# Early bf16 copies of half of w_up, a norm moved to VectorE, FFN state terms moved under mixer tile 2, and a table rule for ScalarE, in a fused decoder layer on 8 cores

## The chip, the cores and the metric

One Trainium2 chip, all 8 cores; each core does one prompt sequence and 16 sample tokens of the batch. The metric is the device time of the slowest core in microseconds. Some executions fall into a slower state in which the cores of a die get a lower clock (972 us here, for a kernel that otherwise takes 830).

## The reference

One layer of a decoder on 2080 tokens per core, width 1024:

```python
h = rmsnorm(x, g_pre_mix);  z = h @ w_in                  # 1024 -> 4096: u, v, B, C, two gates
a = multiscale_pool(u) @ w_pool * scale;  b = (B * causal_dwconv(C * v)) @ w_conv_out
x = x + rmsnorm((sigmoid(ga) * a + sigmoid(gb) * b) @ w_o, g_post_mix)
h = rmsnorm(x, g_pre_ffn)
gate, val = split(causal_dwconv(h @ w_up))                # 1024 -> 5632, state of 2 rows
x = x + rmsnorm((silu(gate) * val) @ w_down, g_post_ffn)
```

Outputs are the tokens and the new states. Weights come in float32 and are used as bf16.

## The kernel before

The kernel runs the mixer over 5 tiles of tokens (0: 512, 1 to 4: 392 columns), then the FFN over 6 tiles of 344 columns. Between them the normalized activations go through DRAM (`h2T`). A Python scheduler lists all operations, orders them for each engine with a model of their durations, and emits fixed instruction streams with semaphores. So a wait on the chip arises where an operation is later than its place in its engine's stream assumes. The norm's sums of squares are small matmuls that the scheduler puts among the others at the time at which it expects their input.

```python
def epi_r(t, q):                       # residual: scale R, add x, square, store y
    ...                                # tiles 0-3: multiply on VectorE, then pool_dma(r, xT.., acc=True)
    act(... Square: XSQ2 <- R)         # tile 4: multiply and add on GpSimd (pool_tt)
    sp_dma(yT[...], R[t]...)           # after every second q
def epi_x(t, k):                       # second norm: h2 = R * g3 * rstd
    if last:                           # tile 4
        act(... r = r * g3, waits for the y store)
        pool_tt(... h = r * rstd)
    else:
        dve(... h = r * g3 * rstd in one scalar_tensor_tensor)
    if k % 4 == 3: sp_dma(h2T[...], H2S[t]...)
def pre_ffn():                         # sample tokens' FFN state terms, at FFN tile 1
    sp_dma(ST_FFN, st_ffn)             # ST_FFN lies over Y
    3 x pool tensor_tensor of 704 columns
def wup(n): ...                        # pool_dma: next n w_up blocks, float32 DRAM -> bf16 SBUF
```

Buffers are laid over each other. What matters below: the residual buffer `R` of tile 1 overlaps that of tile 0, and so does `XSQ2` of tile 1 (its squares), so the output projection of tile 1 (`WO`, evacuated by ScalarE) may not write there before tile 0's `y` store has landed; the FFN's `Y` and `YSQ` lie over tile 4's `R` and `H2S`.

## Time and profile before

| | before |
|---|---|
| fast runs | 829.4 to 831.3 us |
| TensorE busy | 96% of 832.4 us |
| lost by TensorE between 336 and 445 us, mean of 8 cores (largest) | 10.9 us (14.0) |
| the same from 30 to 336 us (mixer) | 0.0 us (0.6) |

"Lost" is used for this sum: for each matmul, the distance from its start to the next one's start, less the usual distance for its width (147 ns at 346 columns, 166 at 392, 210 at 498). It counts waits and half-clock stretches together, in one profiled execution. The page, the stretches, the waits and the chain of the kernel before are shown and read in the prediction.

### The profile page before, as it was taken

The page shows a single profiled execution, that of the slowest core. Times are in us where ns is not written, and L with a number is a line of the kernel's source. Part 1 is how long each engine was busy: PE and PEld are TensorE (multiplying, and loading weights), DVE is VectorE, ACT ScalarE, POOL GpSimd, SP SyncE. Part 2 cuts the span into 40 slices and gives each one's busy share as a digit, 9 for nine tenths or more (in the row PEclk, how much of TensorE's full clock was granted, in tenths as well). Part 3 has the DMA queues.
Part 4 walks back from the last instruction along what each step waited for, and adds up shares of the span by engine and source line. Part 5 has one row for each costly group of instructions (what it writes and reads, how often), then busy time and mean ns, then how long its engine had stood idle before and what let it go on. Part 6 is the DMA issues. An engine that isn't in the chain of part 4 may idle for free.

```text
span 832.4 us, 16714 instructions; the slowest of 8 cores (825.7 to 832.4 us)
## 1 busy us (share of the span) xinstructions
PE 801.2 (96%) x5108; PEld 499.1 (60%) x5108; DVE 556.6 (67%) x1046; ACT 471.8 (57%) x923; POOL 269.0 (32%) x305
## 2 busy tenths in 40 slices
PE   6999999999999999989969999999999999999994
PEld 4455455555555555556646666666666666666662
DVE  2987438876957686578756586658656766685723
ACT  3433386676575646687834475557555654775531
POOL 6432002001002262589662243225212522152231
PEclk9999999999999999999989999999999999999998
DMA  9999706556116999999990033004201500050073
GB/s 171 199 152 157 158 1 154 144 128 140 55 36 155 128 152 196 176 153 168 174 152 1 2 67 37 26 24 62 55 1 35 70 1 1 2 69 2 2 124 82
DMA packets 62838, 75.16 MB, mean 90 GB/s; under 512 B 3072, under 2 KB 59264, under 8 KB 62736
## 3 DMA queue, kind: packets, MB, share of 16 engines
q0 software_dynamic: 41440, 44.97, 39.4%
q1 hardware_dynamic: 21312, 29.14, 13.1%
q8 instruction: 43, 0.70, 0.3%
q14 instruction: 43, 0.35, 0.2%
HBM read 81.53 MB, written 22.90 MB: 125 GB/s over the span
## 4 chain that ended last, share of the span: by engine, by line
PE 88%; DMA 5%; ACT 2%; issue 2%; POOL 2%; DVE 1%; DVEq 0%; ACTq 0%; POOLq 0%; SPq 0%
PE ps L464 88%; DMA big<-xT 2%; DMA h2T<-big 1%; DMA big<-w_up 1%; DVE big L821 1%; POOL big L835 1%; POOL big L477 0%; POOL big L757 0%; ACT big L817 0%; DVEq L1047 0%; DVE big L865 0%; ACT big L941 0%; ACT big L834 0%; ACT big L724 0%; ACT big L848 0%
## 5 line engine op out<-in xcount | busy, mean ns | idle before, releaser
L464 PE MATMUL ps<-big 128*128 128x346 bf16 (+4 forms) x5108 | 801.2, 320 | 19.7 <-ACT big L845 6.5
L464 PEld LDWEIGHTS ps<-big 128*128 128x128 bf16 x5108 | 499.1, 99 | 321.5 <-issue 26.4
L821 DVE SCALAR_TENSOR_TENSOR big<-ps,big 128x344 f32<-128x344 f32 (+1 forms) x528 | 280.4, 569 | 108.5 <-ACT big L817 90.0
L835 POOL TENSOR_TENSOR big<-big 128x344 bf16<-128x344 f32 x132 | 124.9, 949 | 256.5 <-DVE big L821 176.1
L817 ACT ACTIVATE big<-ps,big 128x344 f32<-128x344 f32 (+1 forms) x264 | 138.6, 542 | 65.7 <-PE ps L464 61.2
L834 ACT ACTIVATE big<-big 128x344 f32<-128x344 f32 x132 | 64.3, 489 | 38.5 <-DVE big L821 36.8
L475 POOL DMA_DIRECT2D big<-xT x16 | 15.6, 1011 | 174.7 <-DVE big L707 107.8
L694 ACT ACTIVATE big<-ps 128x392 f32<-128x392 f32 (+1 forms) x80 | 39.0, 514 | 53.4 <-PE ps L464 32.2
L845 ACT ACTIVATE big<-ps,big 128x344 f32<-128x344 f32 x48 | 26.0, 547 | 57.9 <-PE ps L464 55.7
L707 DVE SCALAR_TENSOR_TENSOR big<-ps,big 128x392 f32<-128x392 f32 (+1 forms) x40 | 25.8, 646 | 41.8 <-PE ps L464 41.0
L477 POOL DMA_DIRECT2D big<-w_up x44 | 33.4, 764 | 53.2 <-PE ps L464 47.6
L508 DVE TENSOR_TENSOR big<-big 128x1568 bf16<-128x1568 bf16 (+3 forms) x28 | 22.2, 795 | 31.1 <-ACT big L726 30.1
L475 POOL DMA_DIRECT2D yT<-big x21 | 27.3, 1488 | 32.0 <-DVE big L865 17.2
L851 DVE TENSOR_TENSOR big<-big 128x688 bf16<-128x688 bf16 x17 | 8.8, 517 | 41.9 <-ACT big L848 41.9
L724 ACT ACTIVATE big<-ps,big 128x392 f32<-128x392 f32 (+1 forms) x40 | 24.5, 612 | 17.7 <-PE ps L464 11.1
L848 ACT ACTIVATE big<-ps 128x344 bf16<-128x344 f32 x48 | 21.6, 450 | 18.8 <-PE ps L464 11.1
L603 DVE TENSOR_TENSOR big<-big 128x406 f32<-128x406 f32 (+7 forms) x50 | 30.0, 600 | 3.1 <-ACT big L666 1.1
L477 POOL DMA_DIRECT2D big<-w_in x32 | 23.0, 735 | 21.0 <-DMA big<-w_in 13.5
L575 DVE SCALAR_TENSOR_TENSOR big<-big 128x392 f32<-128x392 f32 (+1 forms) x40 | 25.4, 646 | 2.2 <-ACT big L572 1.6
L713 DVE TENSOR_TENSOR big<-big 128x392 bf16<-128x392 f32 (+1 forms) x40 | 23.1, 587 | 2.4
L711 DVE TENSOR_TENSOR big<-ps,big 128x392 f32<-128x392 f32 (+1 forms) x40 | 23.4, 586 | 1.9 <-ACT big L694 0.4
L572 ACT ACTIVATE big<-big 128x392 f32<-128x392 f32 (+1 forms) x20 | 12.6, 636 | 20.7 <-DVE big L658 20.7
(62 smaller groups left out, 375.6 us busy)
## 6 DMA issues: line engine op xcount, KB each, us to landing
big<-w_up POOLq DMA_DIRECT2D x44, 256.0 KB, 13.1
big<-w_in POOLq DMA_DIRECT2D x32, 256.0 KB, 24.2
yT<-big POOLq DMA_DIRECT2D x21, 344.0 KB, 6.5
big<-xT POOLq DMA_DIRECT2D x16, 392.0 KB, 8.5
yT<-big SPq DMA_DIRECT2D x8, 784.0 KB, 8.7
big<-w_dn POOLq DMA_DIRECT2D x8, 704.0 KB, 20.1
big<-xT SPq DMA_DIRECT2D x6, 784.0 KB, 6.0
big<-h2T SPq DMA_DIRECT2D x6, 692.0 KB, 6.3
```

Source lines behind the costliest of these rows:

```text
L464: ins = e.matmul(o, lhsT=l, rhs=x, start=(start and i == 0), stop=(stop and i == last))
L475: return S.add("pool", lambda e: e.dma_start(out=out, in_=in_, accum_op=ALU.add, max_dma_last_dim=mx), r, w, dma=True, byts=byts, pri=pri, ...
L477: return S.add("pool", lambda e: e.dma_start(out=out, in_=in_, max_dma_last_dim=mx), r, w, dma=True, byts=byts, pri=pri, after=after)
L575: dve(lambda e, k=k: e.scalar_tensor_tensor(out=cv, in0=p[:, 2 + k + lo:2 + k + N], scalar=cc(C_WC + 4 * k + c), in1=cv, op0=ALU.mult, op1 ...
L603: dve(lambda e, nx=nx, cur=cur, s=s, a2=a2: e.tensor_tensor(out=nx[:, a2:W], in0=cur[:, a2:W], in1=cur[:, a2 - s:W - s], op=ALU.add), [ct] ...
L694: act(lambda e, b=b, g=g: e.activation(out=GT[t].ap[:, g, lo:N], in_=bank(b, N, lo), func=AF.Sigmoid), [("ps", b)], [GT[t].t(g, 1)], N, ps ...
L707: dve(lambda e: e.scalar_tensor_tensor(out=A_, in0=bank(bp, N, lo), scalar=cc(C_PS + m), in1=A_, op0=ALU.mult, op1=ALU.mult), [("ps", bp), ...
L817: act(lambda e, b=b, fj=fj, tt=tt: e.activation(out=tt[:, 0:n], in_=bank(b, n), func=AF.Copy, scale=cc(C_WF + fj)), [("ps", b), KCST], [to ...
L821: dve(lambda e, b=b, fj=fj, tt=tt, k=k: e.scalar_tensor_tensor(out=tt[:, 0:n], in0=ps[:, b * 512 + k:b * 512 + k + n], scalar=cc(C_WF + 44 ...
L834: act(lambda e: e.activation(out=g, in_=g, func=AF.Silu), [T.t(0, 1)], [T.t(0, 1)], NB, tab="silu")
L835: S.add("pool", lambda e: e.tensor_tensor(out=gb.ap[:, j, :], in0=g, in1=v, op=ALU.mult), [T.t()], [gb.t(j, 1)], dur=NB * 2.17 + 100)
L845: act(lambda e: e.activation(out=Y.ap[:, m, :], in_=bank(b, NB), func=AF.Copy, scale=cc(C_G4 + m)), [("ps", b), KCST], [Y.t(m, 1)], NB, ps ...
```

## The change

Its intent is to empty the handover from mixer to FFN, where DMA and GpSimd are full, by doing work earlier, where they are idle:

1. 22 of the 44 w_up blocks are cast under tiles 1 to 3 from DRAM to a bf16 scratch in DRAM, and fetched later by SyncE without a cast.
2. Tile 4's second norm goes from ScalarE and GpSimd to VectorE.
3. The FFN state terms are computed under tile 2 instead of FFN tile 1, in another buffer.
4. The scheduler may hold ScalarE up to 0.4 us for an operation of the function table that is loaded (the table rule).

```diff
+NDIR = 22
+                    if c.tab not in (None, tab):
+                        near = [x for x in a if x.tab == tab and ready[x.idx] <= s + 400.0]
+                        if near:
+                            c = min(near, key=lambda x: x.pri + x.off)
+                            s = max(s, ready[c.idx])
...
-    ST_FFN = Buf(Y.off, 44, 2 * NS)
+    ST_FFN = Buf(h2b.off, 44, 2 * NS)
... (in wup: blocks from NDIR on come by sp_dma from wu16)
+    def wcast(n):
+        for _ in range(n):
+            i = cast_next[0]
+            cast_next[0] += 1
+            pool_dma(wu16[:, (i - NDIR) * BL:(i - NDIR + 1) * BL], w_up[:, i * BL:(i + 1) * BL], ...
... (epi_x: the branch for tile 4 is gone; pri=-30000 + 1500 * k if last; epi_n2: flt 6000 -> 2500)
-            if t == NTA - 1:
-                wup(1)
+            if t == L:
+                wup(2)
+            elif t > 0 and m > t and cast_next[0] < 44:      # gates of tiles 1 to 3
+                wcast(1)
...
+    pre_ffn_load()                                           # after the gates of tile 1
     for t in range(2, L):
         for i in range(16):
             F_block(t, i)
+            if i % 2 == 0 and i < 10:                        # projection of tiles 2 and 3
+                wcast(1)
... 
         B(t)
+        if t == 2:
+            pre_ffn()
```

More of the change, by code (lines that the diff above doesn't have):

```diff
@@ L303, in build_nc @@
     h2T = nc.dram_tensor("h2T", [128, KC, NTOK], BF16).ap()
+    wu16 = nc.dram_tensor("wu16", [128, (44 - NDIR) * KC * 128], BF16).ap()
     stack = ExitStack()
@@ L425, in build_nc @@
     H2, G = [h2a, h2b], [g0, g1]
-    ST_FFN = Buf(Y.off, 44, 2 * NS)
-    assert ST_FFN.end <= Y.end
+    ST_FFN = Buf(h2b.off, 44, 2 * NS)
+    assert ST_FFN.end <= PRE.off and R[1].end <= ST_FFN.off + 1600
     TAIL = Buf(h2a.off, 1, 44 * 18)
@@ L492, in wup @@
             k = i + 1
-            while k < hi and W_UP.b[k].off == W_UP.b[k - 1].off + BW:
+            while k < hi and k != NDIR and W_UP.b[k].off == W_UP.b[k - 1].off + BW:
                 k += 1
             dst = Buf(W_UP.b[i].off, 1, (k - i) * BL, True)
-            pool_dma(dst.flat, w_up[:, i * BL:k * BL], [], [dst.t()], 128 * (k - i) * BL * 4, mx=2048,
+            if i < NDIR:
+                pool_dma(dst.flat, w_up[:, i * BL:k * BL], [], [dst.t()], 128 * (k - i) * BL * 4, mx=2048,
+                         after=[last_pe[0]])
+            else:
+                j = i - NDIR
+                sp_dma(dst.flat, wu16[:, j * BL:(j + k - i) * BL], [("wu", b) for b in range(i, k)], [dst.t()],
+                       128 * (k - i) * BL * 2, after=[last_pe[0]])
+            i = k
+    cast_next = [NDIR]
+    def wcast(n):
+        for _ in range(n):
+            i = cast_next[0]
+            cast_next[0] += 1
+            pool_dma(wu16[:, (i - NDIR) * BL:(i - NDIR + 1) * BL], w_up[:, i * BL:(i + 1) * BL], [], [("wu", i)], 128 * BL * 4, mx=2048,
                      after=[last_pe[0]])
-            i = k
     def load_x(t, parts, after=()):
@@ L769, in epi_n2 @@
     def epi_n2(t):
-        rstd(XSQ2[t], 0 if t == NTA - 1 else 2, TA[t], lo_of(t, LO), flt=6000.0 if t == NTA - 1 else 4000.0)
+        rstd(XSQ2[t], 0 if t == NTA - 1 else 2, TA[t], lo_of(t, LO), flt=2500.0 if t == NTA - 1 else 4000.0)
     def epi_x(t, k):
@@ L776, in epi_x @@
         r, h = R[t].ap[:, k, lo:N], H2S[t].ap[:, k, lo:N]
-        if last:
-            act(lambda e: e.activation(out=r, in_=r, func=AF.Copy, scale=cc(C_G3 + k)),
-                [R[t].t(k, 1), KCST, ("y", t, k // 4)], [R[t].t(k, 1)], N, ap=1)
-            pool_tt(lambda e: e.tensor_tensor(out=h, in0=r, in1=SD.ap[:, rs, lo:N], op=ALU.mult),
-                    [R[t].t(k, 1), SD.t(rs, 1)], [H2S[t].t(k, 1)], N)
-        else:
-            dve(lambda e: e.scalar_tensor_tensor(out=h, in0=r, scalar=cc(C_G3 + k), in1=SD.ap[:, rs, lo:N],
-                                                 op0=ALU.mult, op1=ALU.mult),
-                [R[t].t(k, 1), SD.t(rs, 1), KCST], [H2S[t].t(k, 1)], N, stt=True)
+        dve(lambda e: e.scalar_tensor_tensor(out=h, in0=r, scalar=cc(C_G3 + k), in1=SD.ap[:, rs, lo:N],
+                                             op0=ALU.mult, op1=ALU.mult),
+            [R[t].t(k, 1), SD.t(rs, 1), KCST], [H2S[t].t(k, 1)], N, stt=True, pri=-30000 + 1500 * k if last else 0)
         if k % 4 == 3:
@@ L882, in epi_y, with pre_ffn_load @@
                      2 * 128 * 2 * NB * 4, acc=True, mx=4096)
+    def pre_ffn_load():
+        sp_dma(ST_FFN.flat, st_ffn_d, [], [ST_FFN.t()], 128 * 1408 * 4, after=[last_pe[0]])
     def pre_ffn():
-        sp_dma(ST_FFN.flat, st_ffn_d, [], [ST_FFN.t()], 128 * 1408 * 4)
         st = ST_FFN.flat.rearrange("p (c r s) -> p c r s", c=44, r=2)
@@ L890, in pre_ffn @@
         S.add("pool", lambda e: e.tensor_tensor(out=st[:, :, 0, :], in0=st[:, :, 0, :], in1=w0b, op=ALU.mult),
-              [ST_FFN.t(), KCST], [ST_FFN.t()], dur=du)
+              [ST_FFN.t(), KCST], [ST_FFN.t()], dur=du, after=[last_pe[0]])
         S.add("pool", lambda e: e.tensor_tensor(out=st[:, :, 1, :], in0=st[:, :, 1, :], in1=w1b, op=ALU.mult),
-              [ST_FFN.t(), KCST], [ST_FFN.t()], dur=du)
+              [ST_FFN.t(), KCST], [ST_FFN.t()], dur=du, after=[last_pe[0]])
         S.add("pool", lambda e: e.tensor_tensor(out=PRE.ap, in0=st[:, :, 0, :], in1=st[:, :, 1, :], op=ALU.add),
@@ L953, in build_nc @@
         F_block(t, i)
+    L = NTA - 1
     def B(t):
@@ L970, in epi @@
             epi_x(t, k)
-    L = NTA - 1
     B(0)
@@ L987, in build_nc @@
         B(t)
+        if t == 2:
+            pre_ffn()
+    assert cast_next[0] == 44
     for i in range(16):
@@ L1012, in build_nc @@
         if t == 1:
-            pre_ffn()
             assert up_next[0] == 44
```

## The prediction

> **What bounds the kernel now.** I read the page first, then busy time by stretches of 20 us, then TensorE's own waits, then the chain of waits around the worst one. The page says that TensorE is busy 96% of the span, with one dent in the clock it was granted:
>
> ```profile
> span 832.4 us, 16714 instructions; the slowest of 8 cores (825.7 to 832.4 us)
> PE 801.2 (96%) x5108; PEld 499.1 (60%) x5108; DVE 556.6 (67%) x1046; ACT 471.8 (57%) x923; POOL 269.0 (32%) x305
> PEclk9999999999999999999989999999999999999998
> ```
>
> So TensorE is the bound, and only its holes can be won. The stretches show where they are (columns: TensorE, weight loads, VectorE, ScalarE, GpSimd busy us, granted clock, DMA share, GB/s):
>
> ```profile
> 320.00:340.00 20.00, 20.00 (x123) 11.90 (x122) 12.42 (x22) 11.36 (x19) 8.29 (x12) 1.00 1.08 192
> 340.00:360.00 20.00, 19.26 (x130) 12.28 (x128) 13.13 (x26) 16.24 (x30) 8.85 (x12) 1.00 1.09 150
> 360.00:380.00 20.00, 17.84 (x122) 11.52 (x121) 15.13 (x32) 14.29 (x29) 19.68 (x20) 1.00 1.13 154
> 380.00:400.00 20.00, 19.37 (x133) 12.74 (x131) 18.49 (x37) 13.69 (x28) 19.13 (x18) 1.00 1.15 172
> 400.00:420.00 20.00, 19.46 (x131) 12.64 (x132) 15.13 (x31) 17.25 (x35) 13.90 (x16) 1.00 1.07 192
> 420.00:440.00 20.00, 13.48 (x79) 8.17 (x78) 8.36 (x16) 6.81 (x15) 10.73 (x10) 0.83 0.86 111
> ```
>
> From 30 to 340 us (mixer tiles) and from 440 to 780 us (FFN) every stretch is full. Holes are in the start, the last 12 us, and in 340 to 440 us, where the mixer hands over to the FFN: idle there is 0.74 + 2.16 + 0.63 + 0.54 + 6.52 = 10.6 us. After the 6.5 us hole the clock records give half speed for 6.8 us, of which TensorE worked 6.2, so some 3.1 us more are lost: 13.7 us. Summing the matmuls' start distances in the trace over the median distance of their own width gives 14.0 us for this core, and 13.1, 8.9, 9.5, 7.7, 11.7, 8.4, 14.0 for cores 0 to 6. The waits in this stretch:
>
> ```profile
> PE ps L464 <- ACT big L845: 6.5, 1, 6.5
> PE ps L464 <- DMA big<-w_up: 1.6, 1, 1.6
> PE ps L464 <- DVE big L821: 1.3, 4, 0.5
> PE ps L464 <- DVE big L508: 0.6, 1, 0.6
> ```
>
> The longest one, followed back in the chain (start us, us, what) and on ScalarE:
>
> ```profile
> 416.27 0.99 POOL big L780
> ...
> 417.38 12.47 DMA h2T<-big
> ```
>
> ```profile
> 429.93 0.46 ACT L848 ACTIVATE big<-ps 128x344 bf16<-128x344 f32 x1 [7.69 <-DMA h2T<-big]
> ```
>
> L848 is the square that evacuates the first down-projection. It writes a buffer that lies over tile 4's second normalized tile, so it must wait until that tile is stored to DRAM. The store waits for L780, the eight GpSimd multiplies of about 1.0 us that run between 409.7 and 425.0, interleaved with the FFN's own GpSimd products; the second half's store goes out at 425.1 and lands at 429.9. ScalarE stands behind it, PSUM fills, TensorE stops. GpSimd is busy 38.8 of the 40 us before (360 to 400): it is the slow link of the whole tile-4 epilogue.
>
> **What the Trainium skill says.** "TensorE: Matmul & The Clock Gate", section "Part 1: The HAM clock gate", says that the clock falls to half after an idle window of about 3.4 us and returns after a busy one. The trace agrees: hole of 6.52 us, half clock for 6.8 us. Thus removing this hole is worth more than its length. "DMA: Bandwidth & Descriptors", section "SWDGE vs HWDGE vs iDMA", says that a cast during DMA must be issued by GpSimd and that plain copies can go from SyncE; here all casting weight loads are indeed GpSimd issues of about 0.74 us each. "ScalarE: Activation LUTs", section "What ACT_TABLE_LOAD costs", gives 1283 ns for a load; the trace shows 1.28 us.
>
> **The change, part by part.**
>
> *Weights.* 22 of the 44 w_up blocks are cast early into DRAM and fetched by SyncE as bf16. Removed from the GpSimd queue around 300 to 380 us: 22 x 0.74 = 16 us of issue, of which about 7 x 0.74 = 5 us lie in the crowded 360 to 380 us. For DMA: the GpSimd queue moved 44.97 MB in 39.4% of 832 us, 7.3 us of all 16 engines per MB; the SyncE queue 29.14 MB in 13.1%, 3.7 us per MB. 22 blocks of 0.262 MB are 5.8 MB, so 42 us leave the saturated stretch (share 1.07 to 1.15) and 22 come back. Also the loads are issued two at a time in tile 4, so the last ones no longer race the pairs that use them. The 1.6 us wait for w_up (with its neighbours 2.5 us in 360 to 372) goes. Added: 22 casts under tiles 1 to 3. Between 110 and 275 us the DMA share is 0.45, 74 us of 165; plus 42 it is about 0.7. TensorE is full there and has no load to wait for; nothing lies on the path unless the accumulating loads of the residual come late.
>
> *Second norm of tile 4 on VectorE.* Removed: 8 x 1.0 us GpSimd and 8 x 0.62 us ScalarE (L778, which also wait for the y store). Added: the same operation as in the other tiles, 0.622 us each on VectorE by line L783, 8 x 0.622 = 5.0 us, with priority, beside an FFN in which VectorE is busy 18.5 of 20 us (380 to 400).
>
> *State terms.* Three GpSimd products (1.4 + 1.4 + 1.7 = 4.4 us, at 422.7 to 433.5) and a 704 KB load leave the FFN for tile 2, where GpSimd is busy about a tenth of the time. They also leave the region of Y, so Y no longer waits on them.
>
> *Table rule.* After a Ln, the scheduler now waits up to 0.4 us for an Exp of the same table instead of switching. In the first tile-4 norm this saves two loads:
>
> ```profile
> 353.42 1.28 ACT L519 ACT_TABLE_LOAD   x1
> ...
> 356.20 1.28 ACT L834 ACT_TABLE_LOAD   x1
> ...
> 359.25 1.28 ACT L524 ACT_TABLE_LOAD   x1
> ```
>
> With the Exp right after the Ln (which ends at 355.3) the scale is ready at about 355.9 instead of 361.1, 5 us sooner.
>
> *Sum on the path of the hole.* The store that ended at 429.9 comes earlier by 5 us (table rule) + about 5 (weight issues gone from GpSimd) + the L780 stretch, 15.3 us, shrinking to some 6 on VectorE = some 19 us: it lands near 411. The first square was ready to run at 422.2 (429.9 less its wait of 7.69), and by the other holes' 4 us sooner, 418. The margin is 7 us, so I take it that this hole and its half-clock tail go entirely: 6.7 + 2.1 on the slowest core. Of the 14.0 us lost I expect to stay: 1.2 at the entry to the FFN (PSUM waits behind ScalarE's evacuation at 342 to 352, untouched), 0.5 elsewhere, and about 1.5 new, from the VectorE burst: 3.2. Cores' spans less their own loss give a floor of 818.1 to 820.0 (the highest is core 4: 831.7 - 11.7). The slowest core then ends at about 819.7 + 3.2 = 822.9 in the profile; the timed median is 1.1 below the profiled span (831.3 against 832.4), so about 822.
>
> **Rivals.** (1) *VectorE takes over as the bound of the hand-over.* In FFN tile 0 a pair of blocks takes TensorE 16 x 147 ns = 2.35 us and VectorE four times about 0.53 = 2.1 us; 5 us of extra work with priority meets a slack of a tenth, and the PSUM buffers hold some three pairs, 7 us. For: 18.5 of 20 us busy. Against: the items are spread by their priorities, and by 400 to 420 us VectorE is at 15.1. It would leave 4 to 6 us of holes: 825 to 827. (2) *The casts disturb the mixer.* Each sum of squares of a norm stands at a fixed place in TensorE's order, set for expected latencies; a cast of 1.9 us ahead of the accumulating residual load (8.5 us from issue to landing) could hold TensorE a few us per tile: 826 to 832. For: same queue, in order. Against: the casts sit in the first part of each tile and the DMA share stays under 1. (3) *The store's wait is replaced by another*, such as w_dn, which lands 20.1 us after issue, or SyncE loads held in its in-order queue ahead of y and h2 stores. W_dn gains from the emptier queue, so I give it little: 824 to 828. (4) *Everything is hidden*: 818 to 819.
>
> **Range and chances.** All of the gain lies inside 14 us, 1.7% of 831; over 2% would need under 814.7 and some 4 us from the start or the end, which the change doesn't touch. Slower by 2% would need 848, that is holes in the mixer larger than all those of today. I put 822, with 818 to 828 as the range.
>
> **What would show it right or wrong.** Right: in 340 to 440 us TensorE idles under 4 us, the clock stays 1.00 past 30 us, no ScalarE wait for the h2 store near 420 remains, table loads fall below 45, and the GpSimd share in 360 to 400 drops well below 19 of 20. Rival 1: TensorE waits for L821 summing to over 3 us, with the new norm before them on VectorE. Rival 2: stretches between 110 and 340 us with TensorE under 20.00, waiting for a norm's tree sum. Wrong altogether if the span stays above 829, or if TensorE's hole near 427 is still there with another releaser.

## The result

832.41 us median (830.4 to 832.6, 4 runs, all fast) against 830.75 us (four runs, one of them slow; the three fast ones have a median of 830.2): a ratio of 1.002, 95% interval 0.9996 to 1.0044. Ratios here are the mean time of one kernel's fast runs over that of the other's fast runs of the same rounds, so not quite the ratio of the quoted medians. The kernel is no faster; I had predicted 822, with 828 as the upper end. The page after:

```profile
span 831.1 us, 16766 instructions; the slowest of 8 cores (823.0 to 831.1 us)
PE 799.8 (96%) x5108; PEld 498.3 (60%) x5108; DVE 568.1 (68%) x1054; ACT 451.5 (54%) x902; POOL 259.7 (31%) x294
PEclk9999999999999999999999999999999999999998
```

The dent in the granted clock is gone from the page, and yet TensorE's share is the same. The stretches of the slowest core, 4 (same columns as in the prediction):

```profile
160.00:180.00 20.00, 18.30 (x109) 10.38 (x107) 18.90 (x34) 7.33 (x14) 0.04 (x1) 1.00 1.29 159
180.00:200.00 20.00, 16.14 (x80) 8.75 (x81) 7.75 (x14) 13.91 (x28) 0.00 (x0) 0.83 0.71 161
...
220.00:240.00 20.00, 17.55 (x107) 10.18 (x106) 19.31 (x30) 7.20 (x16) 5.67 (x6) 1.00 0.99 158
...
360.00:380.00 20.00, 20.00 (x138) 13.31 (x136) 16.66 (x34) 15.96 (x30) 14.34 (x13) 1.00 0.25 85
380.00:400.00 20.00, 20.00 (x139) 13.35 (x137) 18.38 (x35) 14.52 (x29) 19.57 (x18) 1.00 1.03 155
400.00:420.00 20.00, 18.98 (x130) 12.46 (x129) 19.14 (x38) 14.06 (x27) 10.42 (x12) 1.00 1.14 191
420.00:440.00 20.00, 20.00 (x138) 13.36 (x137) 16.67 (x32) 10.84 (x23) 6.32 (x8) 1.00 0.55 101
```

The handover is nearly full: one hole of 1.0 us is left, and 420 to 440 us went from 13.48 busy at clock 0.83 to 20.00 at 1.00. The mixer, full before, now has two holes on this core, with a clock dent after the first. Per core, the mean loss in the handover fell from 10.9 to 1.2 us, and the mean loss in the mixer rose from 0.0 to 7.7 us (3.6 to 11.4). So the expected gain arrived, and most of it was spent elsewhere. By these sums the change still wins 2 us in the mean, and the times do not show it: the profiled run before was 3.3 us above its kernel's median (834.0 against 830.75), the one after lay at its own (832.62 against 832.41). TensorE's waits from 30 to 340 us on this core:

```profile
PE ps L471 <- ACT big L747: 5.5, 1, 5.5
PE ps L471 <- DVE big L529: 2.5, 1, 2.5
PE ps L471 <- ACT big L958: 1.9, 1, 1.9
```

(The third lies in the start of the kernel, around 29 us, and is there in other runs too.) **Hole one**, 5.5 us at 178 us: in the chain of waits and on ScalarE,

```profile
142.03 15.42 DMA big<-xT
...
157.53 25.55 DMA yT<-big
```

```profile
183.22 0.50 ACT L747 ACTIVATE big<-ps 128x392 bf16<-128x392 f32 x1 [12.11 <-DMA yT<-big]
```

L747 writes tile 1's squares, in the evacuation of its output projection. It waited 12.1 us for tile 0's `y` store, since the squares lie over tile 0's `R`. The store took 25.6 us, after an accumulating load of x that took 15.4; before, the longest of tile 0's accumulating loads on core 4 took 12.6 and the longest SyncE transfer issued beside them 9.1. The hole's length varies: 170 to 200 us loses 0.9 to 8.6 us on seven cores and nothing on core 5. Issues between 130 and 172 us on core 4 and their median time to landing, before and after:

```profile
big<-xT POOLq DMA_DIRECT2D x4, 498.0 KB, 9.9
yT<-big SPq DMA_DIRECT2D x2, 996.0 KB, 7.8
```

```profile
wu<-w_up POOLq DMA_DIRECT2D x11, 256.0 KB, 27.0
big<-xT POOLq DMA_DIRECT2D x4, 498.0 KB, 10.7
yT<-big SPq DMA_DIRECT2D x2, 996.0 KB, 22.6
```

Eleven of the early casts were issued in these 42 us, and themselves took 27 us to land. **Hole two**, 2.5 us at 223 us, has the same length on all cores (2.5 us of waiting, 2.6 by the sum), which speaks against DMA timing. On cores 2, 3, 5 and 6 a stretch of half clock of 3.4 us follows, so that they lose 4.0 to 4.3 us there. TensorE waits for L529, a tree sum (adds on VectorE ahead of a norm's sum of squares). VectorE and GpSimd just before it:

```profile
217.31 4.37 DVE L734 TENSOR_TENSOR big<-big 128x392 bf16<-128x392 f32 x2
221.60 2.86 DVE L529 TENSOR_TENSOR big<-big 128x1568 bf16<-128x1568 bf16 x1
```

```profile
217.77 1.39 POOL L907 TENSOR_TENSOR big<-big 128x704 f32<-128x704 f32 x1
219.10 0.72 POOL L484 DMA_DIRECT2D wu<-w_up  x1
219.84 1.40 POOL L909 TENSOR_TENSOR big<-big 128x704 f32<-128x704 f32 x1
221.17 0.73 POOL L484 DMA_DIRECT2D wu<-w_up  x1
221.92 1.70 POOL L911 TENSOR_TENSOR big<-big 128x704 f32<-128x704 f32 x1
```

Each L734 usually takes 0.57 us; these two take 2.29 and 2.16. The tree's first step usually takes 0.97 us and here 2.86. That is (2.29 + 2.16 - 2 x 0.57) + (2.86 - 0.97) = 5.2 us more. Each ends about 0.4 to 0.9 us after one of the three state products (L907, L909, L911) on GpSimd. The Trainium skill says in "SBUF — State Buffer", section "SBUF: two separate sides", that GpSimd and VectorE share a port pair as an exclusive lock, and that a VectorE operation takes part in it if it has two SBUF inputs. The slow operations have two SBUF inputs; whether an operation with one operand in PSUM keeps its time beside a product is seen in the next runs, since none stands beside one here. I had looked at this change without looking that up.

### The profile page after: what moved, and what is told of

Its sections match the earlier page's. It is cut to its first block, busy times and chain, and to the rows that moved or that the text cites. A ratio compares the mean times of both kernels' runs of the same rounds, so it can differ in the third digit from the quotient of the medians.

```text
span 831.1 us, 16766 instructions; the slowest of 8 cores (823.0 to 831.1 us)
## 1 busy us (share of the span) xinstructions
PE 799.8 (96%) x5108; PEld 498.3 (60%) x5108; DVE 568.1 (68%) x1054; ACT 451.5 (54%) x902; POOL 259.7 (31%) x294
## 3 DMA queue, kind: packets, MB, share of 16 engines
q1 hardware_dynamic: 23760, 34.90, 15.4%
## 4 chain that ended last, share of the span: by engine, by line
PE 86%; DMA 7%; DVE 2%; ACT 1%; issue 1%; POOL 1%; DVEq 0%; ACTq 0%; POOLq 0%; SPq 0%
PE ps L471 86%; DMA big<-xT 4%; DMA yT<-big 3%; DVE big L529 1%; DVE big L836 1%; DVE big L734 0%; ACT big L555 0%; POOL big L484 0%; DVEq L1072 0%; DVE big L880 0%; ACT big L958 0%; DVE big L732 0%; POOL big L850 0%; DVE big L798 0%; ACT big L783 0%
## 5 line engine op out<-in xcount | busy, mean ns | idle before, releaser
L836 DVE SCALAR_TENSOR_TENSOR big<-ps,big 128x344 f32<-128x344 f32 (+1 forms) x528 | 281.7, 570 | 100.6 <-ACT big L832 77.4
L529 DVE TENSOR_TENSOR big<-big 128x1568 bf16<-128x1568 bf16 (+3 forms) x28 | 25.0, 895 | 29.2 <-ACT big L747 27.4
L484 POOL DMA_DIRECT2D wu<-w_up x22 | 15.4, 698 | 93.6 <-PE ps L471 86.8
L747 ACT ACTIVATE big<-ps 128x392 bf16<-128x392 f32 (+1 forms) x40 | 21.3, 536 | 13.2 <-DMA yT<-big 12.1
L734 DVE TENSOR_TENSOR big<-big 128x392 bf16<-128x392 f32 (+1 forms) x40 | 26.4, 669 | 2.3
```

What stands on the lines that cost most here:

```text
L484: return S.add("pool", lambda e: e.dma_start(out=out, in_=in_, max_dma_last_dim=mx), r, w, dma=True, byts=byts, pri=pri, after=after)
L529: dve(lambda e, w=w: e.tensor_tensor(out=sq.ap[:, 0:w, 0:n], in0=sq.ap[:, 0:w, 0:n], in1=sq.ap[:, w:2 * w, 0:n], op=ALU.add), [sq.t(0, 2 * ...
L734: dve(lambda e: e.tensor_tensor(out=MERGED[t].ap[:, m, lo:N], in0=A_, in1=B_, op=ALU.add), [G_.t(ga, 1), G_.t(gb, 1)], [MERGED[t].t(m, 1)], N)
L836: dve(lambda e, b=b, fj=fj, tt=tt, k=k: e.scalar_tensor_tensor(out=tt[:, 0:n], in0=ps[:, b * 512 + k:b * 512 + k + n], scalar=cc(C_WF + 44 ...
```

## The experiments

Theory A: the early casts crowd the DMA queues while tile 0's residual is loaded and stored, and tile 1's evacuation waits (hole one). Theory B: the state products on GpSimd hold up VectorE products of two SBUF operands (hole two). Rivals: the new order of instructions (table rule), or the mere amount of work (on VectorE for hole two, of casts for hole one). The first eight kernels start from the changed kernel, the last four from the kernel before. All gave correct results. Losses are means of 8 cores of the profiled run (largest core in brackets). One profile is one execution: that of the kernel before was 3.3 us above the median, that of direct weights with the old table rule 2.5 us below.

| kernel | median us | ratio to before (95%) | lost in mixer | lost in handover |
|---|---|---|---|---|
| before | 830.8 | | 0.0 (0.6) | 10.9 (14.0) |
| after | 832.4 | 1.002 (0.9996 to 1.0044) | 7.7 (11.4) | 1.2 (1.3) |
| after, direct weights | 824.9 | 0.993 (0.992 to 0.994) | 0.2 (0.5) | 2.2 (3.9) |
| after, state in FFN | 828.4 | 0.997 (0.995 to 0.999) | 3.6 (7.1) | 1.8 (1.9) |
| after, both of these | 828.0 | 0.996 (0.994 to 0.998) | 0.4 (1.7) | 3.3 (5.2) |
| after, state on VectorE | 827.4 | 0.996 (0.994 to 0.998) | 2.3 (7.3) | 1.2 (1.8) |
| after, late casts | 826.2 | 0.994 (0.992 to 0.996) | 3.3 (4.4) | 0.8 (1.4) |
| **after, late casts, state on VectorE** | 824.0 | **0.990 (0.988 to 0.992)** | 0.2 (0.5) | 0.7 (1.2) |
| direct weights, old table rule | 828.6 | 0.996 (0.995 to 0.998) | 0.6 (0.9) | 3.1 (5.0) |
| direct weights, old norm | 826.5 | 0.994 (0.992 to 0.996) | 0.2 (0.5) | 3.4 (5.3) |
| before + casts | 829.4 | 0.998 (0.996 to 1.000) | 3.3 (7.5) | 1.2 (2.8) |
| before + norm on VectorE | 828.0 | 0.995 (0.993 to 0.997) | 0.1 (0.6) | 3.3 (8.1) |
| before + table rule | 829.9 | 0.998 (0.996 to 1.000) | 0.2 (0.7) | 4.6 (8.1) |
| before + state under tile 2 | 825.7 | 0.993 (0.992 to 0.995) | 1.0 (3.1) | 1.7 (3.6) |

(Medians count slow runs, ratios do not. Over fast runs alone the medians are 830.2 before, 827.7 for both, 825.9 for the old norm, 827.6 for the norm alone, and 822.6 for the best row, whose four fast runs are 821.7, 822.5, 822.7 and 825.3.)

**Direct weights.** Edit: `NDIR = 44`, so no scratch and no early cast; `wup(2)` kept.

> The changed kernel with all 44 w_up blocks cast straight into SBUF as before (no scratch, no early casts), everything else of the change kept. Theory A (the early casts crowd the DMA queue in the first mixer tiles, the store of y of tile 0 lands late and TensorE stops near 178 us): that hole (1.3 to 5.6 us, with the half clock after it up to 8 us on the slow cores) is gone on all cores, the hole of 2.6 us near 218 us stays, loss between 30 and 340 us falls from 3.6 to 11.4 us per core to about 2.5; time about 824 us, if the old wait for w_up stays away, 826 if it comes back. Rival (the hole near 178 us comes from the new order of instructions, not from DMA load): hole stays, time 830 to 832.

Hole one is gone on all eight cores (170 to 200 us: -0.03 us each), as theory A says, and the `y` store lands in 9.5 us on core 4. But hole two went as well, against my expectation. The stretching is there still:

```profile
208.94 2.25 DVE L734 TENSOR_TENSOR big<-big 128x392 bf16<-128x392 f32 x2
211.11 2.06 DVE L529 TENSOR_TENSOR big<-big 128x784 bf16<-128x784 bf16 x1
```

The two L734 take 584 and 1744 ns instead of 567 each, and this tree step of 784 elements 2057 instead of 555: 2.7 us extra, where the full change had 5.2. With no casts issued between them, GpSimd's three products follow each other closely, and the first runs beside VectorE operations with a PSUM operand, which keep their times:

```profile
207.72 1.38 POOL L907 TENSOR_TENSOR big<-big 128x704 f32<-128x704 f32 x1 [11.67 <-PE ps L471]
```

```profile
207.93 0.62 DVE L728 SCALAR_TENSOR_TENSOR big<-ps,big 128x392 f32<-128x392 f32 x1
208.46 0.56 DVE L732 TENSOR_TENSOR big<-ps,big 128x392 f32<-128x392 f32 x1
```

That 5.2 us extra made a hole of 2.6 us speaks for some 2.6 us of slack ahead of TensorE's sums, which 2.7 us would just use up; but VectorE's steps also stand in another order here, so this is an inference, not a measurement.

**State terms back in the FFN.**

```diff
-    ST_FFN = Buf(h2b.off, 44, 2 * NS)
+    ST_FFN = Buf(Y.off, 44, 2 * NS)
-        if t == 2:
-            pre_ffn()
         if t == 1:
+            pre_ffn_load()
+            pre_ffn()
```

> The changed kernel with the FFN state terms back in FFN tile 1 (their load over Y again), casts kept. Theory B (the three GpSimd products under tile 2 hold up VectorE's products of two SBUF operands): the hole of 2.6 us near 218 us is gone on every core and the long VectorE products (2.15 to 2.86 us) are 0.57 and 0.97 us again, the hole near 178 us stays; time 828 to 830. Rival (VectorE is slowed by the casts that GpSimd issues between the products): long products and the hole stay. Second question: whether a hole near 415 us comes back because Y waits for the state terms; I expect less than 2 us of it.

Hole two is gone on every core (200 to 240 us: -0.04), on core 4 no L734 takes over 0.68 us and no L529 over 1.23, though the casts are still issued. So the products are needed for it. Hole one stayed (up to 6.9 us on core 6), and on core 4 the crowding appeared in another form: a wait of 3.0 us for the tree of a norm, before 170 us: there one accumulating load took 20.1 us, and the sums came late. In the FFN the same products run beside L836, which reads PSUM, and L836 keeps 0.56 to 0.58 us. Only tile 4's norm L798, with two SBUF operands, is stretched there, from 0.62 to between 0.79 and 1.56 us.

**Both undone.** Edits of the two runs above together.

> Both parts undone: what remains is VectorE's second norm of tile 4, the table rule and w_up two blocks at a time. If theories A and B name all of the loss: no hole over 0.5 us between 30 and 340 us, handover 340 to 440 us under 4 us of loss, time 819 to 823, faster than before by 1.0 to 1.4%. If the early casts are needed for the handover, the w_up wait of 1.6 us or more returns near 365 us and the time is 823 to 826.

A miss: 828.0 (827.7 over fast runs) instead of 819 to 823. Mixer losses are 0.4 us, so theories A and B do name the mixer's loss, but the handover loses 3.3 us (5.2): on core 4 TensorE waits 2.1 us for the tree of tile 4's norm (L529) and 2.2 us for evacuations (L747, L836). Moving the state terms thus has a value of its own.

**State products on VectorE**, at the same place in the program:

```diff
-        S.add("pool", lambda e: e.tensor_tensor(out=st[:, :, 0, :], ...
+        S.add("dve", lambda e: e.tensor_tensor(out=st[:, :, 0, :], ...      # all three
```

> The changed kernel with the three state products at the same place in the program but on VectorE. Theory B (lock between a GpSimd operation and a VectorE operation with two SBUF operands): three VectorE operations of about 0.9 us each are added, no VectorE product of 392 elements takes over 0.7 us, and the hole near 218 us shrinks below 1.5 us. Rival (simply too much work ahead of the tree at that place): 2.7 us on VectorE give a hole of 2 us or more. The hole near 178 us stays in both; time 828 to 831.

Each product takes 0.88 us on VectorE instead of 1.4 to 1.7 on GpSimd, and 200 to 240 us loses nothing (-0.04 on all cores). No L734 takes over 0.57 us, no L529 over 0.97. So 2.7 us more work on VectorE makes no hole there, against the rival, and the stretching needs the products on GpSimd. That the port lock is what stretches is the skill's account: the pattern of operands fits it in every run looked at, but no run changes the lock alone. The time is just under my range. Hole one stays on core 4 (6.8 us), on two cores it is absent.

**Late casts.** The 22 casts moved away from tile 0's residual:

```diff
-            elif t > 0 and m > t and cast_next[0] < 44:
+            elif cast_next[0] < 44 and ((t == 2 and m in (0, 1, 7)) or (t == 3 and m < 5)):
-            if i % 2 == 0 and i < 10:
+            if (t == 2 and i in (9, 11, 13)) or (t == 3 and i % 3 != 2):
```

> The changed kernel with the 22 early casts moved: none before or beside the residual loads and the y store of tile 0; three late in tile 2's projection, three in its gates, eleven in tile 3's projection, five at the head of its gates. Nothing else changed. Theory A (what hurts is where the casts stand, not that they exist): the y store of tile 0 lands again in about 9 us instead of 21, no hole near 178 us over 0.7 us on any core, time 823 to 826. Rival (22 casts cost what they cost wherever they stand, because the DMA engines are too slow for them): a hole of several us turns up later, near 240 or 270 us, time over 828. The GpSimd products of the state terms stay; their hole near 218 us should be between 0 and 2.6 us depending on what stands behind them.

Hole one is gone everywhere (170 to 200 us: -0.03); hole two stays with 2.4 us (4.1 on two cores), and casts stand between the products here too. The time is just outside my range. So for hole one the place of the casts matters, not their number.

**Late casts and state products on VectorE**, the two edits together.

> As the run before with the state products on VectorE. If both named causes are right, no hole over 0.7 us is left between 30 and 340 us, the handover loses about 1.2 us as in the changed kernel; time 821 to 823.5, the best so far. If it is not better than the direct weights (824.9), the early casts buy nothing that direct loading has not.

The mixer loses 0.2 us, the handover 0.7; the mean of the fast runs lies in my range. The landing times of before are back; core 4, 130 to 172 us:

```profile
yT<-big SPq DMA_DIRECT2D x2, 996.0 KB, 9.6
...
wu<-w_up POOLq DMA_DIRECT2D x3, 256.0 KB, 3.9
```

This kernel beats both: 1.0% faster than before (0.988 to 0.992). Its fast runs average 823.0 us, against 824.9 of direct weights in other rounds on another chip; relative to before it is 0.990 against 0.993, with intervals that overlap slightly, so that early casts buy anything over direct loading is likely but not settled.

**Direct weights, old table rule** (the five added scheduler lines taken out):

> Direct weights (no casts) and in addition the old table rule. If the table rule shortens the epilogue of tile 4 by some 5 us as I predicted and that matters, a hole of a few us returns between 400 and 440 us and the time is 826 to 830; if VectorE's norm alone removed the hole, the time stays at 824 to 826. Table loads: 45 with the old rule.

In range, but the place was wrong: 400 to 440 us loses nothing, 380 to 400 loses 1.2 to 4.1. It has 47 table loads against 32. The rule is worth about 0.3% there (0.996 against 0.993, from two chips' rounds).

**Direct weights, old norm** (the branch for tile 4 and `flt=6000` put back):

> Direct weights (no casts), table rule kept, tile 4's second norm back on ScalarE and GpSimd. If the norm on VectorE is what removed the store's wait, the ScalarE wait for the store of h2 and a hole of 3 to 7 us near 420 us return, time 828 to 832; if the table rule and the state terms' move had done it, no hole there and 824 to 826.

826.5 (825.9 over fast runs) lies near the second of my two forecasts, with 0.5 to 2.2 us lost between 400 and 440 us on seven cores. The norm on VectorE was not what the long hole hung on alone.

**One part alone, from the kernel before.** The edits are the parts 1 to 4 as in the diff, each with the rest of the kernel before.

> The kernel before with the weights part alone: early casts of 22 blocks at the places of the change, w_up two blocks at a time in tile 4. Theory A: the y store of tile 0 lands in about 21 us instead of 9 and a hole of 1 to 6 us opens near 178 us, as in the changed kernel; the wait for w_up near 365 us goes. With no state products under tile 2 no hole near 218 us. The h2 store's hole near 427 us shrinks but stays in part, since the norm is on GpSimd: time 828 to 835. Rival: the hole near 178 us is made by the table rule's new order; then there is none here.

> The kernel before with tile 4's second norm on VectorE alone. By my prediction's sum this part took 9 of the 19 us by which the store had to come earlier, with 7 us to spare, so alone it should nearly close the hole near 427 us (6.7 us and its half clock) and leave the wait for w_up: 824 to 827.

> The kernel before with the scheduler's table rule alone. The first norm of tile 4 gets its scale 5 us sooner; that is less than the 7.7 us that ScalarE waited, but saved table loads (32 instead of 45) also relieve ScalarE, so the hole near 427 us should shrink to 0 to 3 us: 824 to 829.

> The kernel before with the state terms moved under tile 2 alone, loads cast directly. The lock makes some VectorE products of two SBUF operands last 1.2 to 2.1 us instead of 0.57 and 0.97; with no casts issued between the GpSimd products no hole over 1 us follows near 210 us. In the FFN GpSimd has 4.4 us less to do and Y is free sooner, but the h2 store still waits for the norm on GpSimd: hole near 427 us 2 to 5 us, time 826 to 830.

Casts alone: the `y` store lands in 20 to 21 us on cores 4, 6 and 7, and 170 to 200 us loses 0.7 to 5.2 us. The table rule isn't there, so it isn't the cause of hole one; nor is there a hole two. The handover falls to 1.2 us, better than I expected. Norm alone and table rule alone leave 3.3 and 4.6 us; both times are 0.6 to 1 us above their ranges (fast runs), and part of the old hole is still there (400 to 440 us: 1.0 to 5.1 us with the norm, 1.0 to 6.2 with the rule). The state terms alone are worth most of the four, 0.7%, a little faster than I expected, with a mixer loss of only 0.66 us in 200 to 240 us, although one operation of the kind of L734 takes 1.74 us and one tree step 2.47.

## Why the prediction was wrong

- **What bounds it, and the size of the prize.** Right in place. TensorE's losses in the handover fell by 9.7 us in the mean, to 1.2 where I expected 3.2, but from the profile of a long execution (834.0 us). The late casts with state products on VectorE ran 822 to 825 us: the 822 could be had, but not by this change.
- **The step that failed first: "nothing lies on the path unless the accumulating loads of the residual come late".** I added 42 us of DMA work to a mean share of 0.45 and got 0.7, under 1. The mean was the wrong reading. Core 4 already had shares of 1.08 and 0.93 between 140 and 160 us, in which tile 0's four accumulating loads and 2 MB of stores stand, and half of the casts were issued between 132 and 160 us: the share became 1.16 to 1.33 from 150 to 180 us. The last load was late, 15.4 us against at most 12.6 before, but most of the delay came in what followed it, the `y` store (25.6 us) and the buffers shared with tile 1. Casts alone cost 3.3 us in the mean, up to 7.5.
- **The step that failed second: the state terms go where "GpSimd is busy about a tenth of the time".** I priced 4.4 us of GpSimd and asked only whether GpSimd was free. The cost fell on VectorE, 5.2 us, on steps that read two SBUF operands; in the FFN, beside the same products, L836 with one operand in PSUM kept its time. By itself this hardly costs anything (0.66 us); with casts between the products it is a hole of 2.4 to 2.6 us on every core, and 4.0 to 4.3 us with the half clock that follows on four cores of the change and two with late casts.
- **A term of the sum that was mis-sized: "the timed median is 1.1 below the profiled span".** I set one execution's span against the median of others. Every execution is timed 1.5 to 1.6 us above its own slowest core's span (before: 834.0 against 832.4), so my 822.9 in the profile meant about 824.5. This explains some 2.6 of the 10 us by which I missed.
- **The half clock.** In the prediction TensorE "worked 6.2" of the 6.8 us at half clock; the trace has 4.26, so some 2.1 us were lost there and not 3.1 (the later sum has 2.1), and that 13.7 came close to 14.0 was luck. Nor does the length of a standstill alone decide: in the kernel before, 3.8 and 3.9 us on cores 2 and 4 left no half clock, in the changed one about 2.5 us did on cores 2, 3, 5 and 6.
- **The sum on the path of the hole** (19 us earlier, 7 to spare) was right in direction, yet it hid that the parts overlap: each of the four alone takes the handover from 10.9 to between 1.2 and 4.6 us. The long hole stood on a thin margin. What each part does there in detail, and why the casts alone do as much as all four, I have not separated.
- **Rivals.** Rival 2 was the right one (I gave it 826 to 832). The wait that I named, for a norm's tree sum, is that of hole two, but there GpSimd's products made it; in hole one the casts made another wait, for the `y` store. My reason against it, that the DMA share stays under 1, was wrong. Of rival 1 there is 1.0 us for L529 and no wait for L836. The class (same) was right, the range was not: its upper end, 828, left out most of what I had written for rival 2.
- **Signs named beforehand.** Table loads fell from 45 to 32 and the store's wait was gone, as I said. TensorE idled 1.2 us in 340 to 440. GpSimd fell to 14.34 of 20 us in 360 to 380 but stayed at 19.57 in 380 to 400. The clock did not stay at 1.00 past 30 us (0.83 in 180 to 200), and the span, 831.1 us, stayed above the 829 that I had called wrong altogether.

## What to carry to other kernels

Before work is moved into a gap, read that gap at the grain of the work: DMA share by 10 us and the landing time of the stores that buffers wait on, not the mean over a phase. Ask of moved GpSimd work not only whether GpSimd is idle but what VectorE reads at that place. And when several parts all shorten one wait, try each alone: here any one of the four closed more than half of it.

## What the Trainium skill lacked or had wrong

- "SBUF — State Buffer", section "SBUF: two separate sides", states the lock, but no page gives times in microseconds for a VectorE product beside a GpSimd product. The runs show products of 0.57 us taking 1.74 to 2.29 us and a tree step of 0.97 us taking 2.86 beside GpSimd products of 1.4 to 1.8 us. The page says that the one which starts first gets the ports; one VectorE product has a recorded start 0.46 us ahead of the GpSimd product and still ended 0.44 us after it (a cast's issue on GpSimd had begun 0.24 us before it). Recorded spans on GpSimd are rough, so this is a question and not a refutation. That the hole is larger where issues stand between the products (2.4 to 2.6 us with, 0.7 or none without) is on no page; the order of VectorE's steps differs between these runs too, so the issues are not shown to be the cause.
- "DMA: Bandwidth & Descriptors", section "Issuing engines are not separate DMA queues", says that queues interleave on the same engines, but gives no figure for a store beside a stream of casts between two DRAM tensors: 8 to 10 us to landing became 20 to 23 in the changed kernel, and a 256 KB cast itself took 22 to 28 us there (medians of cores 4, 6 and 7) against 4 where it met no such store.
- "ScalarE: Activation LUTs", section "What ACT_TABLE_LOAD costs", adds about 1.38 us of drain to the 1283 ns of a table load. Here the load starts 0.02 us after the operation before it has ended and the next begins 0.01 us after the load (356.18, 356.20, 357.49 us): a switch cost 1.31 us.
- "TensorE: Matmul & The Clock Gate", section "Back-to-back issue gap", gives about 131 ns as the sustained distance of matmuls of 512 columns in a real kernel. Here it was 216 ns at 512 (runs of eight), and in long streams 166 at 392 and 147 at 346 columns, with a weight load each, which is what the page calls the isolated gap. No page has a single standstill shorter than the 3.4 us quoted in the prediction with half clock after it; here one of 2.5 us had that on four cores of eight.
